# A hybrid attention and FFN block on one core: squares of one x tile divided anew, output projection through scratch tiles, merge gates at a later place

## The chip, the cores and the metric

The kernel runs on 1 core of one Trainium2 chip. The metric is the time of one execution on the device in microseconds (us). Before the change the median of 3 runs is 1706.45 us (1705.3 to 1707.63). One more execution was profiled; the times of single instructions come from it. TensorE is called PE in the profile (PEld is its weight load), VectorE DVE, ScalarE ACT, GpSimd POOL, and SP is the engine whose queue issues most of the DMAs.

## The reference

One layer over 256 latent tokens `x` and 256 context tokens `ctx`, all in float32, with a model width of 2048. Cut to what matters:

```python
hc = modulate(rms_norm(ctx, norm1_g), m_ctx[0], m_ctx[1])          # adaLN of the context tokens
h  = modulate(rms_norm(x, norm1_g), m_lat[0], m_lat[1])            # adaLN of the latent tokens
pc = hc @ w_in[:, :KV_WIDTH];  p = h @ w_in                        # keys, values; queries and gates for x only
oa = gqa(qa, ka_all, va_all);  ob = diff_attn(qb, kb_all, vb_all, ...)
merged = sigmoid(ga) * (oa @ w_br_a) + sigmoid(gb) * (ob @ w_br_b)
x2  = x + m_lat[2] * (merged @ w_out)
h2  = modulate(rms_norm(x2, norm2_g), m_lat[3], m_lat[4])
out = x2 + m_lat[5] * ((silu(h2 @ w_ff_gate) * (h2 @ w_ff_up)) @ w_ff_down)
```

`rms_norm(x)` is `x * rsqrt(mean(x*x) + eps) * g`, and the `m_...` are the six chunks of `silu(c) @ w_ada + b_ada`.

## The kernel before, in words

**Products.** Each weight tile (128x1024 float32, called `wraw`) is split into a high part `whi` (rounded to fp32r by a cast on ScalarE, L227) and a low part `wlo` (the rest, a subtraction on VectorE, L229). Each product is three matmuls (`mm3`, L233 to L235): activation high with weight high, high with low, low with high. There are 7 `wraw` buffers and 3 each of `whi` and `wlo`; a `wraw` buffer comes free when VectorE has made the low part, and SP then issues the next load into it. The instructions of an engine run in the order in which they stand in its queue. The order is decided before the run by a scheduler that works from the program's order and from `issue_after(...)`, which holds an instruction back behind a named one.

**First stage.** Tokens come as four tiles of 128x2048: tile 2 and 3 are x, 0 and 1 are ctx. `row_norm(i)` (L126) sums the squares of a tile: ScalarE squares the middle half (128x1024, L130), VectorE the first and the last quarter (128x512 each, L133); VectorE adds the sums (L136), GpSimd raises them to the power -0.5 (L137), VectorE scales the first 128 columns (L139). TensorE turns these columns (`turn_first`, `xtp`, L351), ScalarE applies scale and shift and so makes the high part of the first activation tile (L364), VectorE the low part (L365, L366), and `kv_first` multiplies it with the first rows of w_in (L374, L375, L377). `hold(cg)` splits the weights for that. `keep_busy(n)` (L345) issues n transposes of the identity whose result nobody reads. Behind the first stage, blocks of the adaLN vectors (`ada`, L290) alternate with matmul groups: an `ada` sum is copied (`asb`, L294), turned (`atp`, L299), and gives scale and shift for the next activation tiles (L331 to L335).

**Merge.** The gates were multiplied out during attention and parked in DRAM (`gate_d`). For each of four column groups `cg`, `load_gated` loads them (`gin`), puts them through a sigmoid on ScalarE (L912) and multiplies (L915), while `project(w_bra, ...)` runs its eight steps of two weight tiles' rows; `take(gates, 1)` moves the generator on by one in each step. In the first column group the end of attention still runs: `o` (L790, copied at L784), and `o_parts(3)`, which makes the last `oT` tiles (L238, L239).

**Output projection.** `out_evac(cg)` takes the two finished token tiles: `y = ps * a2` (L966), `y += xr` (L967), the square sum on ScalarE (L969), and a write of y to DRAM (`x2_d`, L970, GpSimd's queue). y stands in the tile `xn`. `scaled` (L982) then multiplies y by the row `s2`, in place for column groups 0 to 2 and into a scratch tile `z` for group 3; it is called three steps into the next projection. `norm2` applies the row norm to all four quarters (L991), TensorE turns them (`htp`, L996), and the FFN begins. In column group 3 the first six weight tiles of the FFN's gate are loaded and split as well (`first_weights`, into `wbig` tiles or `whi` and `wlo`).

## Time and profile before

| | |
|---|---|
| median of 3 runs | 1706.45 us |
| lowest, highest | 1705.3, 1707.63 us |
| the profiled execution | 1708.76 us |
| its span, first to last instruction | 1707.0 us |
| TensorE busy | 1683.8 us (99%) |
| VectorE, ScalarE, GpSimd busy | 1146.4, 768.8, 201.0 us |
| DMA | 413.15 MB, mean 242 GB/s |
| mean granted TensorE clock | 0.998 |

The profiled execution lies 1.76 us above its span and 2.31 us above the median. In rows of a timeline the first number is the start in us from the span's start, the second the duration; then engine, line, operation, what it writes and reads, how many; in brackets the idle time of the engine before it and who ended that. A row of a table of windows gives the window, its length, the busy time of PE, PEld, DVE, ACT and POOL (with the instruction count), the granted clock, the busy share of the DMA engines, and GB/s.

### The profile page before, as it was taken

The page shows a single profiled execution, that of the slowest core. Times are in us where ns is not written, and L with a number is a line of the kernel's source. Part 1 is how long each engine was busy: PE and PEld are TensorE (multiplying, and loading weights), DVE is VectorE, ACT ScalarE, POOL GpSimd, SP SyncE. Part 2 cuts the span into 40 slices and gives each one's busy share as a digit, 9 for nine tenths or more (in the row PEclk, how much of TensorE's full clock was granted, in tenths as well). Part 3 has the DMA queues.
Part 4 walks back from the last instruction along what each step waited for, and adds up shares of the span by engine and source line. Part 5 has one row for each costly group of instructions (what it writes and reads, how often), then busy time and mean ns, then how long its engine had stood idle before and what let it go on. Part 6 is the DMA issues. An engine that isn't in the chain of part 4 may idle for free.

```text
span 1707.0 us, 21494 instructions
## 1 busy us (share of the span) xinstructions
PE 1683.8 (99%) x7893; PEld 1354.3 (79%) x7893; DVE 1146.4 (67%) x1460; ACT 768.8 (45%) x1037; POOL 201.0 (12%) x295
## 2 busy tenths in 40 slices
PE   7999999999999999999999999999999999999999
PEld 4677778887887778887888788888888888888887
DVE  4764779788788878996666755566666666554554
ACT  4222223246656556577544544444444444433332
POOL 0200002011031110001111101111111111100000
PEclk9999999999999999999999999999999999999999
DMA  8787795678757668676787857788888888765662
GB/s 322 271 294 271 260 338 168 211 260 264 249 177 219 224 225 281 234 246 205 249 270 234 294 173 222 226 268 270 263 268 270 265 273 255 237 221 192 217 209 89
DMA packets 180139, 413.15 MB, mean 242 GB/s; under 512 B 14880, under 2 KB 16112, under 8 KB 179776
## 3 DMA queue, kind: packets, MB, share of 16 engines
q1 hardware_dynamic: 167760, 374.23, 67.0%
q0 software_dynamic: 12272, 37.53, 7.2%
q8 instruction: 62, 1.02, 0.2%
q14 instruction: 45, 0.37, 0.1%
HBM read 395.42 MB, written 16.29 MB: 241 GB/s over the span
## 4 chain that ended last, share of the span: by engine, by line
PE 88%; DVE 5%; DMA 2%; ACT 2%; issue 2%; POOL 0%; SPq 0%; DVEq 0%; ACTq 0%
PE mm L233 27%; PE mm L234 27%; PE mm L235 27%; PE ada L290 2%; DVE wlo L229 1%; DMA wraw<-in_w_in_dram 1%; PE ptp L769 1%; PE o L790 1%; ACT whi L227 1%; PE s L745 1%; ACT p L694 1%; DVE nr L483 0%; DMA wada<-in_ada_t_dram 0%; DMA gate_d<-gate 0%; DVE mx L691 0%
## 5 line engine op out<-in xcount | busy, mean ns | idle before, releaser
L229 DVE TENSOR_TENSOR wlo<-wraw,whi 128x1024 fp32r<-128x1024 f32 x498 | 607.2, 1221 | 420.6 <-ACT whi L227 419.6
L227 ACT CAST whi<-wraw 128x1024 fp32r<-128x1024 f32 x498 | 523.1, 1051 | 730.5 <-PE mm L235 593.1
L234 PE MATMUL mm<-wlo,hT 128*128 128x512 f32 x684 | 266.2, 389 | 0.1
L233 PE MATMUL mm<-whi,hT 128*128 128x512 f32 x684 | 266.1, 389 | 0.0
L235 PE MATMUL mm<-whi,hT 128*128 128x512 f32 x684 | 266.1, 389 | 0.0
L233 PE MATMUL mm<-whi,xT 128*128 128x512 f32 x630 | 251.8, 403 | 1.1 <-DVE vb L418 0.4
L234 PE MATMUL mm<-wlo,xT 128*128 128x512 f32 x630 | 246.9, 392 | 1.0 <-DVE wlo L229 1.0
L235 PE MATMUL mm<-whi,xT 128*128 128x512 f32 x630 | 246.1, 391 | 0.0
L435 DVE SCALAR_TENSOR_TENSOR ada<-wada,vt,ada 128x1024 f32<-128x1024 f32 x120 | 152.1, 1278 | 0.0
L234 PEld LDWEIGHTS mm<-wlo,hT 128*128 128x128 f32 x684 | 128.4, 188 | 27.3 <-DVE wlo L229 0.5
L233 PEld LDWEIGHTS mm<-whi,hT 128*128 128x128 f32 x684 | 128.4, 188 | 26.7
L235 PEld LDWEIGHTS mm<-whi,hT 128*128 128x128 f32 x684 | 128.4, 188 | 26.3
L233 PEld LDWEIGHTS mm<-whi,xT 128*128 128x128 f32 x630 | 117.8, 188 | 38.5 <-issue 10.8
L234 PEld LDWEIGHTS mm<-wlo,xT 128*128 128x128 f32 x630 | 118.5, 188 | 26.0 <-DVE wlo L229 2.9
L235 PEld LDWEIGHTS mm<-whi,xT 128*128 128x128 f32 x630 | 118.3, 188 | 25.2
L233 PE MATMUL mm<-whi,fT 128*128 128x512 f32 x354 | 137.5, 388 | 0.5 <-DVE y L1088 0.5
L235 PE MATMUL mm<-whi,fT 128*128 128x512 f32 x354 | 137.3, 388 | 0.0
L234 PE MATMUL mm<-wlo,fT 128*128 128x512 f32 x354 | 137.3, 388 | 0.0
L233 PEld LDWEIGHTS mm<-whi,fT 128*128 128x128 f32 x354 | 66.4, 188 | 15.0 <-issue 0.8
L235 PEld LDWEIGHTS mm<-whi,fT 128*128 128x128 f32 x354 | 66.4, 188 | 13.8
L234 PEld LDWEIGHTS mm<-wlo,fT 128*128 128x128 f32 x354 | 66.5, 188 | 13.7
L233 PE MATMUL mm<-whi,oT 128*128 128x512 f32 x192 | 75.9, 396 | 0.0
(242 smaller groups left out, 2148.1 us busy)
## 6 DMA issues: line engine op xcount, KB each, us to landing
wraw<-in_w_in_dram SPq DMA_DIRECT2D x159, 512.0 KB, 4.8
wada<-in_w_ada_dram SPq DMA_DIRECT2D x128, 512.0 KB, 4.8
wraw<-in_w_ff_gate_dram SPq DMA_DIRECT2D x88, 512.0 KB, 4.6
wraw<-in_w_ff_up_dram SPq DMA_DIRECT2D x88, 512.0 KB, 5.2
wraw<-in_w_ff_down_dram SPq DMA_DIRECT2D x88, 512.0 KB, 4.7
wada<-in_ada_t_dram SPq DMA_DIRECT2D x64, 512.0 KB, 6.1
wraw<-in_w_br_a_dram SPq DMA_DIRECT2D x32, 512.0 KB, 5.2
wraw<-in_w_out_dram SPq DMA_DIRECT2D x32, 512.0 KB, 5.2
```

The lines of the kernel that those rows point to most:

```text
L227: last_hi.append(nc.scalar.copy(out=hi[:, 0:nk], in_=raw[:, 0:nk]))
L229: last_lo.append(nc.vector.tensor_tensor(out=lo[:, 0:nk], in0=raw[:, 0:nk], in1=hi[:, 0:nk].bitcast(F32), op=ALU.subtract))
L233: nc.tensor.matmul(ps, lhsT=ah, rhs=wh, start=first, stop=False, skip_group_check=skip)
L234: nc.tensor.matmul(ps, lhsT=ah, rhs=wl, start=False, stop=False, skip_group_check=skip)
L235: return nc.tensor.matmul(ps, lhsT=al, rhs=wh, start=False, stop=last, skip_group_check=skip)
L290: last_pe[0] = nc.tensor.matmul(aps[32 * g:32 * g + 32, 0:ncol], lhsT=cst[:, k, :], rhs=rhs, start=(k < 4), stop=(k >= NKT - 4))
L435: nc.vector.scalar_tensor_tensor(out=dst, in0=wt, scalar=sc[:, 0, kt:kt + 1], in1=dst, op0=ALU.mult, op1=ALU.add)
L694: nc.scalar.activation(out=p, in_=sp, func=AF.Exp, bias=mx, accum_out=rs)
L745: nc.tensor.matmul(sps[i], lhsT=qT[rows, x, hh, tk * P:(tk + 1) * P], rhs=kT["b", grp][y][rows, hh, :], start=(n == 0), stop=(n == 2))
L769: nc.tensor.transpose(out=tp[:, kt * P:(kt + 1) * P], in_=p[:, kt * P:(kt + 1) * P], identity=ident)
L790: nc.tensor.matmul(op[:, 0:BV], lhsT=pT[:, kt, :], rhs=vb[:, kt, hh * BV:(hh + 1) * BV], start=(kt == 0), stop=(kt == 3))
```

## The change

1. **First stage.** `row_norm` is divided into `squares_act`, `squares_dve` and the rest. For tiles 2, 0 and 1 the same pieces are squared by the same engines as before. For tile 3 (the second x tile) ScalarE squares the last three quarters (128x1536) and VectorE only the first (128x512); this one is held behind the low part of `hold(2)`, and the low part of `hold(4)` behind it. The second `keep_busy(6)` after the first products becomes `keep_busy(4)`.
2. **Merge.** In column group 0 the sigmoids are held behind the last copy of `o` (a new list `last_o`) and not behind the last high part, and the generator of the gates is moved on by 0, 0, 0, 0, 2, 2, 3, 0 in the eight steps of the projection. The other column groups are as before.
3. **Output projection.** y stands in a scratch tile (tag `nr`, 2 buffers) and not in `xn`; `scaled` reads it and writes `xn`, in all four column groups, 4 ticks after the evacuation for groups 0 to 2 and at once for group 3. `z` goes; `norm2` reads and writes `xn` alone. The square's unused output takes a buffer of tag `sq`.

The change moves instructions at three places that the prediction speaks of. The rows are those of an engine's queue, in order; the numbers in the names tell tiles apart.

The first place is the first stage. On VectorE, `wlo_210` belongs to `hold(2)`, `wlo_214` (now `wlo_216`) to `hold(4)`, `tok3` is the second x tile, `junk` takes the squares that nobody reads, `sums` holds the sums of squares, and `vb0` takes the product of column group 4 for the first x tile. Before:

```order
L229 TENSOR_TENSOR wlo_210<-wraw_181,whi_209 128x1024
L229 TENSOR_TENSOR wlo_214<-wraw_183,whi_213 128x1024
L133 SCALAR_TENSOR_TENSOR junk_245,sums_90<-tok3_185 128x512
L133 SCALAR_TENSOR_TENSOR tok3_185,sums_90<-tok3_185 128x512
L136 TENSOR_REDUCE sums_90<-sums_90 128x1
L382 COPY vb0_105<-mm_227 128x512
L139 TENSOR_SCALAR tok3_185<-tok3_185,sums_90 128x128
```

and after:

```order
L235 TENSOR_TENSOR wlo_210<-wraw_181,whi_209 128x1024
L136 SCALAR_TENSOR_TENSOR junk_213,sums_90<-tok3_185 128x512
L235 TENSOR_TENSOR wlo_216<-wraw_183,whi_215 128x1024
L142 TENSOR_REDUCE sums_90<-sums_90 128x1
L145 TENSOR_SCALAR tok3_185<-tok3_185,sums_90 128x128
L388 COPY vb0_105<-mm_230 128x512
```

One square of `tok3` is gone from VectorE, the other stands ahead of the second low part, and the scaling of `tok3` stands ahead of the copy into `vb0`. On ScalarE, further on in the same stage, `asb_534` (now `asb_531`) is the 256 columns wide `ada` sum of the block after next, and `xT0` and `cT` are the high parts that the next matmul group multiplies. Before:

```order
L227 CAST whi_562<-wraw_560 128x512
L294 COPY asb_450<-ada_429 128x128
L334 ACTIVATE xT0_205<-hx_459,mod0_426 128x256
L334 ACTIVATE cT_458<-hx_463,mod0_426 128x256
L294 COPY asb_534<-ada_509 128x256
```

and after:

```order
L233 CAST whi_559<-wraw_557 128x512
L300 COPY asb_447<-ada_426 128x128
L300 COPY asb_531<-ada_506 128x256
L340 ACTIVATE xT0_205<-hx_456,mod0_423 128x256
L340 ACTIVATE cT_455<-hx_460,mod0_423 128x256
```

The copy of this sum has moved ahead of the two high parts. Its two transposes `atp` have moved likewise on TensorE, from behind the 60 matmuls that follow to a place ahead of them.

The second place is the merge, on ScalarE, in column group 0. `gin` are the gates under the sigmoid, `pT` the turned attention weights, `o1` the last attention output, `oT3` its high part, and the three `whi` are those of steps 3 to 5 of the projection (counted from 0). Before:

```order
L912 ACT_TABLE_LOAD
L912 ACTIVATE gin_7261<-gin_7261 128x512
L238 CAST pT_7177<-ptp_7213 128x4x128
L238 CAST pT_7177<-ptp_7220 128x4x128
L912 ACTIVATE gin_7283<-gin_7283 128x512
L227 CAST whi_7311<-wraw_7309 128x1024
L784 COPY o1_6782<-o_7247 128x512
L227 CAST whi_7331<-wraw_7329 128x1024
L238 CAST oT3_7303<-o1_6782 128x1024
L912 ACTIVATE gin_7327<-gin_7327 128x512
L227 CAST whi_7353<-wraw_7351 128x1024
L912 ACTIVATE gin_7349<-gin_7349 128x512
```

and after:

```order
L233 CAST whi_7297<-wraw_7295 128x1024
L244 CAST pT_7174<-ptp_7210 128x4x128
L244 CAST pT_7174<-ptp_7217 128x4x128
L233 CAST whi_7319<-wraw_7317 128x1024
L796 COPY o1_6779<-o_7242 128x512
L924 ACT_TABLE_LOAD
L924 ACTIVATE gin_7315<-gin_7315 128x512
L244 CAST oT3_7292<-o1_6779 128x1024
L924 ACTIVATE gin_7337<-gin_7337 128x512
L233 CAST whi_7344<-wraw_7342 128x1024
L924 ACTIVATE gin_7360<-gin_7360 128x512
L924 ACTIVATE gin_7364<-gin_7364 128x512
```

Two high parts of weights have moved ahead of the table load and the first two sigmoids; the table load and a sigmoid now stand between the copy of `o1` and `oT3`, and the other two sigmoids behind the high part of step 5.

The third place is the output projection, on VectorE, where column group 2 is evacuated and group 3 runs. `wbig` are the weight tiles that are split into large tiles, the last three of them weights of the FFN. Before:

```order
L229 TENSOR_TENSOR wlo_8502<-wraw_8499,whi_8501 128x1024
L229 TENSOR_TENSOR wbig_8557<-wraw_8555,wbig_8557 128x1024
L229 TENSOR_TENSOR wlo_8522<-wraw_8519,whi_8521 128x1024
L982 TENSOR_TENSOR xn0_7943<-xn0_7943,s2_8293 128x512
L982 TENSOR_TENSOR xn1_7944<-xn1_7944,s2_8293 128x512
L229 TENSOR_TENSOR wlo_8534<-wraw_8531,whi_8533 128x1024
L229 TENSOR_TENSOR wbig_8568<-wraw_8566,wbig_8568 128x1024
L229 TENSOR_TENSOR wlo_8546<-wraw_8543,whi_8545 128x1024
L229 TENSOR_TENSOR wbig_8588<-wraw_8586,wbig_8588 128x1024
L229 TENSOR_TENSOR wbig_8593<-wraw_8591,wbig_8593 128x1024
L229 TENSOR_TENSOR wbig_8598<-wraw_8596,wbig_8598 128x1024
L966 TENSOR_TENSOR xn0_7943<-mm_8461,a2_8457 128x512
```

and after:

```order
L235 TENSOR_TENSOR wlo_8505<-wraw_8502,whi_8504 128x1024
L983 TENSOR_TENSOR xn0_7940<-y2_8446,s2_8294 128x512
L983 TENSOR_TENSOR xn1_7941<-y2_8454,s2_8294 128x512
L235 TENSOR_TENSOR wlo_8525<-wraw_8522,whi_8524 128x1024
L235 TENSOR_TENSOR wbig_8560<-wraw_8558,wbig_8560 128x1024
L235 TENSOR_TENSOR wlo_8537<-wraw_8534,whi_8536 128x1024
L235 TENSOR_TENSOR wbig_8571<-wraw_8569,wbig_8571 128x1024
L235 TENSOR_TENSOR wlo_8549<-wraw_8546,whi_8548 128x1024
L235 TENSOR_TENSOR wbig_8591<-wraw_8589,wbig_8591 128x1024
L235 TENSOR_TENSOR wbig_8596<-wraw_8594,wbig_8596 128x1024
L235 TENSOR_TENSOR wbig_8601<-wraw_8599,wbig_8601 128x1024
L976 TENSOR_TENSOR y2_8582<-mm_8464,a2_8460 128x512
```

The two multiplications by `s2` (into `xn0`, `xn1`) have moved up by two rows of weights, and read `y2`.

The diff:

```diff
         last_pow.append(nc.gpsimd.tensor_tensor(out=r, in0=r, in1=neghalf[:, 0:n], op=ALU.pow))
         return r
-    def row_norm(i, late=None):
-        xt = tok_in[i]
-        mid, end = xt[:, CG:3 * CG], xt[:, 3 * CG:]
-        with tc.issue_after(late[0].ins) if late else nullcontext():
+    def squares_act(i, c0=CG, c1=3 * CG, late=None):
+        mid = tok_in[i][:, c0:c1]
+        with tc.issue_after(late.ins) if late else nullcontext():
             nc.scalar.activation(out=mid, in_=mid, func=AF.Square, scale=D ** -0.5, accum_out=ssq[:, i, 0:1])
-        with tc.issue_after(late[1].ins) if late else nullcontext():
-            for n, (src, dst) in enumerate(((xt[:, 0:CG], scratch("junk", tag="p", bufs=4)), (end, end))):
-                nc.vector.scalar_tensor_tensor(out=dst, in0=src, scalar=1.0 / D, in1=src, op0=ALU.mult, op1=ALU.mult,
-                                               accum_out=ssq[:, i, 1 + n:2 + n])
+
+    def squares_dve(i, parts=(0, 3), late=None):
+        with tc.issue_after(late.ins) if late else nullcontext():
+            for n, q in enumerate(parts):
+                src = tok_in[i][:, q * CG:(q + 1) * CG]
+                dst = src if q else scratch("junk", tag="p", bufs=4)
+                held = nc.vector.scalar_tensor_tensor(out=dst, in0=src, scalar=1.0 / D, in1=src, op0=ALU.mult, op1=ALU.mult,
+                                                      accum_out=ssq[:, i, 1 + n:2 + n])
+        return held
+
+    def row_norm(i):
         r = r_tok[:, i:i + 1]
         nc.vector.tensor_reduce(out=r, in_=ssq[:, i, :], axis=AX.X, op=ALU.add)
         last_pow.append(nc.gpsimd.tensor_tensor(out=r, in0=r, in1=neghalf[:, 0:1], op=ALU.pow))
-        xt = xt[:, 0:P]
+        xt = tok_in[i][:, 0:P]
         nc.vector.tensor_scalar(out=xt, in0=xt, scalar1=r, scalar2=None, op0=ALU.mult)
     r_of = []
...
     BATCH = ((), (1, 4), (0, 1, 2, 3), (0, 1, 2, 3), (0, 1, 2, 3), ())
     steps = STEPS
+    squares_act(2)
+    squares_dve(2)
     row_norm(2)
     turn_first(2)
     keep_busy(6)
...
     keep_busy(6)
     mod_first(2)
     hold(2, (last_asb[-1], last_first[-1]))
-    hold(4, (first_hi[-1], last_first[-1]))
+    hold(4, (first_hi[-1], squares_dve(3, (0,), last_lo[-1])))
+    squares_act(3, CG, 4 * CG, last_hi[-1])
     kv_first(2, (2, 3))
     kv_first(2, (4, 5))
-    keep_busy(6)
+    keep_busy(4)
     for tok, todo in ((3, ((2, (0,)), (3, (2, 3)), (3, (4, 5)), (3, (0,)))),
                       (0, ((0, (2, 3)), (0, (4, 5)), (0, (0,)))), (1, ((1, (2, 3)), (1, (4, 5)), (1, (0,))))):
-        row_norm(tok, (last_hi[-1], last_lo[-1]))
+        if tok < 2:
+            squares_act(tok, late=last_hi[-1])
+            squares_dve(tok, late=last_lo[-1])
+        row_norm(tok)
         with tc.issue_after(last_pe[0].ins):
             turn_first(tok)
         mod_first(tok)
...
         nc.vector.scalar_tensor_tensor(out=p0, in0=p0, scalar=r0, in1=p1, op0=ALU.mult, op1=ALU.add)
         return [p0]
-    pair = []
+    pair, last_o = [], []
     def back(br, u, pr):
...
             for kt in range(4):
                 vh, vl = [v[:, kt, grp * AD:(grp + 1) * AD] for v in v_a]
                 mm3(op, vh, vl, pT[0][:, kt, :], pT[1][:, kt, :], kt == 0, kt == 3)
-            nc.scalar.copy(out=o_raw(grp * 4 + hh - 1, 2), in_=op)
+            last_o.append(nc.scalar.copy(out=o_raw(grp * 4 + hh - 1, 2), in_=op))
             return
         vb = acc["vb"][grp].rearrange("p (t c) -> p t c", c=CG)
         tk = u % 2
...
                     g = scratch("gin", tag="p", bufs=4)
                     nc.gpsimd.dma_start(out=g, in_=gate_d[w, tk, :, cg * CG:(cg + 1) * CG])
                     yield None
-                    with tc.issue_after(last_hi[-1].ins):
+                    with tc.issue_after((last_hi if cg else last_o)[-1].ins):
                         nc.scalar.activation(out=g, in_=g, func=AF.Sigmoid)
                     if w == 1:
                         with tc.issue_after(last_lo[-1].ins):
...
                 if k == 3:
                     assert not work
                     o_parts(3)
-            take(gates, 1)
+            take(gates, 1 if cg else (0, 0, 0, 0, 2, 2, 3, 0)[k])
     drain(later)
     b_all = ada_everywhere("b_all", 2)
...
         nc.gpsimd.dma_start(out=r, in_=row_d[i, cg:cg + 1, :].partition_broadcast(P).rearrange("p l d -> p (l d)"))
         return r
-    s_of = {}
-
     def out_evac(cg):
         a2 = row_piece("a2", 0, cg)
-        s_of[cg] = row_piece("s2", 1, cg)
+        s2 = row_piece("s2", 1, cg)
         def f(tk, ps):
             xr = scratch("xr", tag="p", bufs=4)
             nc.gpsimd.dma_start(out=xr, in_=t["x"][0, tk * P:(tk + 1) * P, cg * CG:(cg + 1) * CG])
-            y = xn[tk][:, cg * CG:(cg + 1) * CG]
+            y = scratch("y2", tag="nr", bufs=2)
             nc.vector.tensor_tensor(out=y, in0=ps, in1=a2, op=ALU.mult)
             nc.vector.tensor_tensor(out=y, in0=y, in1=xr, op=ALU.add)
-            junk = scratch("junk_x")
+            junk = scratch("junk_x", tag="sq", bufs=2)
             nc.scalar.activation(out=junk, in_=y, func=AF.Square, accum_out=ssx[tk][:, cg:cg + 1])
             nc.gpsimd.dma_start(out=x2_d[tk, :, cg * CG:(cg + 1) * CG], in_=y)
-            if cg == 3:
-                scaled(tk, 3)
+
+            def scaled():
+                nc.vector.tensor_tensor(out=xn[tk][:, cg * CG:(cg + 1) * CG], in0=y, in1=s2, op=ALU.mult)
+
+            if cg < 3:
+                after(4, scaled)
+            else:
+                scaled()
         return f
     hT = Parts("hT", NKT)
-    rows, last_norm = {}, []
-
-    def scaled(tk, q):
-
-        y = xn[tk][:, q * CG:(q + 1) * CG]
-        rows[tk, q] = scratch("z") if q == 3 else y
-        nc.vector.tensor_tensor(out=rows[tk, q], in0=y, in1=s_of[q], op=ALU.mult)
+    last_norm = []
     def norm2(tk):
...
         nc.vector.tensor_reduce(out=ss, in_=ssx[tk], axis=AX.X, op=ALU.add)
         r = rstd_of(ss, 1, D, "rstd2")
         for q in range(4):
-            h = rows[tk, q]
+            h = xn[tk][:, q * CG:(q + 1) * CG]
             nc.vector.scalar_tensor_tensor(out=h, in0=h, scalar=r, in1=b_all[:, q * CG:(q + 1) * CG], op0=ALU.mult, op1=ALU.add)
         yield None
         for q in range(4):
             tp = tp_ps("htp") if q % 2 == 0 else s_ps("htp")
             for j in range(4):
-                nc.tensor.transpose(out=tp[:, j * P:(j + 1) * P], in_=rows[tk, q][:, j * P:(j + 1) * P], identity=ident)
+                nc.tensor.transpose(out=tp[:, j * P:(j + 1) * P], in_=xn[tk][:, q * CG + j * P:q * CG + (j + 1) * P], identity=ident)
             hi, lo = hT.four(q, tk * P, P)
             last_norm.append(split(hi, lo, tp.rearrange("p (h q) -> p h q", h=4)))
             yield None
...
             take(norm2_of[1], 2)
     for cg in range(4):
-        gen = project(w_out, mT, NKT, cg * CG, out_evac(cg), **(dict(tail=TURN2, hook=tail_hook, in_big=(6, 7)) if cg == 3 else {}))
-        take(gen, 3)
-        if cg:
-            for tk in range(2):
-                scaled(tk, cg - 1)
-        drain(gen)
+        drain(project(w_out, mT, NKT, cg * CG, out_evac(cg), **(dict(tail=TURN2, hook=tail_hook, in_big=(6, 7)) if cg == 3 else {})))
     NFT = DFF // P
```

## The prediction

> **What bounds the kernel now.** The first line of the profile's page, busy time by engine, says that little is left:
>
> ```profile
> PE 1683.8 (99%) x7893; PEld 1354.3 (79%) x7893; DVE 1146.4 (67%) x1460; ACT 768.8 (45%) x1037; POOL 201.0 (12%) x295
> ```
>
> TensorE is busy for 1683.8 of 1707.0 us. A change that leaves the matmuls alone can win only its 23.2 us of idle time, and time in which its clock is low. So I read the windows around TensorE's waits at the places of the change. Columns: window, length, busy time of PE, PEld, DVE, ACT, POOL, granted clock, DMA share, GB/s.
>
> ```profile
> 20.38:23.84 3.46, 1.60 (x11) 1.04 (x9) 2.34 (x9) 1.72 (x5) 0.55 (x1) 1.00 1.06 410
> 48.29:48.58 0.29, 0.00 (x1) 0.01 (x1) 0.11 (x2) 0.29 (x2) 0.00 (x0) 1.00 1.28 325
> 62.82:63.13 0.31, 0.31 (x3) 0.14 (x1) 0.31 (x2) 0.00 (x0) 0.00 (x0) 1.00 0.18 53
> 802.58:803.47 0.89, 0.00 (x2) 0.03 (x1) 0.89 (x3) 0.89 (x3) 0.46 (x1) 1.00 0.79 276
> 964.40:968.00 3.60, 2.21 (x9) 1.21 (x8) 3.60 (x4) 1.62 (x2) 0.55 (x1) 1.00 1.01 358
> ```
>
> TensorE idles 1.86 us in the first stage, 0.89 in the merge and 1.39 in the output projection. The second and third rows belong to a side effect, below. The last reading is the granted clock, in windows of the first stage:
>
> ```profile
> 14.87:18.28 3.41, 2.21 (x16) 1.40 (x11) 1.78 (x6) 3.03 (x5) 0.00 (x0) 1.00 1.01 398
> ...
> 21.69:25.10 3.41, 1.59 (x6) 1.17 (x7) 2.39 (x6) 2.28 (x5) 0.39 (x1) 1.00 1.04 399
> 25.10:28.51 3.41, 3.41 (x9) 2.65 (x8) 2.14 (x8) 1.85 (x4) 0.55 (x1) 0.50 1.02 410
> ```
>
> From 25.10 to 28.51 us the clock is 0.50 while TensorE has work throughout: 3.41 us at half speed lose 1.70. In the stretch of equal length ahead of it TensorE was busy for 1.59 us (47%); a stretch with 2.21 (65%) did not lower the clock. The waits there are thus paid twice. [...]
>
> **The change part by part.**
>
> *First stage, VectorE.* Its rows around the second x tile (`tok`), then TensorE's and ScalarE's:
>
> ```profile
> 17.61 2.35 DVE L229 TENSOR_TENSOR wlo<-wraw,whi 128x1024 fp32r<-128x1024 f32 x2
> 19.88 0.69 DVE L133 SCALAR_TENSOR_TENSOR junk<-tok 128x512 f32<-128x512 f32 x1
> ...
> 21.29 0.16 DVE L136 TENSOR_REDUCE sums<-sums 128x1 f32<-128x4 f32 x1
> 21.36 0.68 DVE L382 COPY vb<-mm 128x512 f32<-128x512 f32 x1
> 22.11 0.29 DVE L139 TENSOR_SCALAR tok<-tok,sums 128x128 f32<-128x128 f32 x1
> ```
>
> ```profile
> 20.37 0.62 PE L377 MATMUL mm<-wlo,xT 128*128 128x512 f32 x2
> 20.83 0.81 PE L345 MATMUL idle<-ident 128*128 128x128 f32 x6
> 22.46 0.33 PE L351 MATMUL xtp<-ident,tok 128*128 128x128 f32 x1 [0.81 <-DVE tok L139]
> 23.84 0.50 PE L374 MATMUL mm<-whi,xT 128*128 128x512 f32 x1 [1.05 <-ACT whi L227]
> ```
>
> ```profile
> 17.75 1.06 ACT L130 ACTIVATE tok<-tok 128x1024 f32<-128x1024 f32 x1
> 18.72 0.19 ACT L130 ACTIVATION_READ_ACCUMULATOR tok<-tok 128x1 f32 x1
> 19.42 1.07 ACT L384 COPY kb<-mm 128x512 f32<-128x512 f32 x2 [0.52 <-PE mm L377]
> ```
>
> Of two squares VectorE keeps one. It lies between the low parts, so the second low part ends 0.69 later, at 20.65 and not 19.96, and the sum can start there and not at 21.29: 0.64 earlier. Scaling and `xtp` follow as before (0.82 and 0.35 behind), so `xtp` starts at 21.82 and everything that follows it, up to L374 now at 23.84, is 0.64 earlier. TensorE must be free by then: its two L377 wait for the second low part until 20.7 (0.33 late), and four idle transposes take 0.59 instead of 0.81, so they end at 21.75. The copy into `vb`, now behind the scaling, waits for nothing new and ends before VectorE's next step, which waits for ScalarE anyway. On ScalarE 1.5 times 1024 columns cost at most 1.59 instead of 1.06; the 0.53 lie in the 0.52 us for which it waits ahead of the copies at 19.42, so I cost them at nothing (0.1 if that wait were gone). Together **-0.64**, between -0.3 (if the late L377 weighed in full) and -0.8.
>
> *First stage, clock.* The 1.86 us of waits shrink to 0.33 for the low part, some 0.07 ahead of `xtp`, and the unchanged 1.05: 1.45. The worst 3.41 us stretch then has 1.96 of work, 57%, between the 47% that lowered the clock and the 65% that did not. I take it that the clock stays up, being the nearer bound: **-1.70** in an execution like the profiled one; the other end is 0.
>
> *First stage, a side effect.* The copy of the 256 columns wide sum now stands ahead of two high parts on ScalarE.
>
> ```profile
> 48.02 0.51 ACT L334 ACTIVATE xT<-hx,mod 128x256 fp32r<-128x256 f32 x1 [1.74 <-DVE hx L331]
> 48.43 0.49 ACT L334 ACTIVATE cT<-hx,mod 128x256 fp32r<-128x256 f32 x1
> 48.83 0.35 ACT L294 COPY asb<-ada 128x256 f32<-128x256 f32 x1
> ```
>
> It waits for TensorE's sums, which end at 48.29 (start of the idle window above). Then the copy runs, and the high part `xT` starts at about 48.6, not 48.02. The matmuls behind it, and VectorE's low parts, which now also have the reduction of the transposes ahead of them, start some 0.59 later. The two transposes fit into that wait, so their 0.31 us at 62.82 are saved: net **+0.28**, between 0 and +0.6.
>
> *Merge.* ScalarE's rows, and one of TensorE:
>
> ```profile
> 798.85 1.28 ACT L912 ACT_TABLE_LOAD   x1
> 801.36 0.63 ACT L912 ACTIVATE gin<-gin 128x512 f32<-128x512 f32 x1 [1.23 <-DMA gin<-gate_d]
> ...
> 806.97 0.59 ACT L784 COPY o<-o 128x512 f32<-128x512 f32 x1 [2.55 <-PE o L235]
> 807.45 1.05 ACT L227 CAST whi<-wraw 128x1024 fp32r<-128x1024 f32 x1
> 808.40 1.05 ACT L238 CAST oT<-o 128x1024 fp32r<-128x1024 f32 x1
> 809.35 0.64 ACT L912 ACTIVATE gin<-gin 128x512 f32<-128x512 f32 x1
> ```
>
> ```profile
> 812.66 0.39 PE L234 MATMUL mm<-wlo,oT 128*128 128x512 f32 x1
> ```
>
> Before, the table load and the wait for the gate's transfer hold ScalarE, and behind them `pT`, for which TensorE waits 0.89. This wait goes. What is late next? The table load now stands behind the copy of `o`, which TensorE releases at about 806.3 (0.89 earlier than so far, but 0.23 later since its last matmul now follows one more of the projection's; two L377 take 0.62, one L234 0.39). Then come the copy 0.48, table load 1.28, sigmoid 0.6, `oT` 0.95, sigmoid 0.6, the high part of step 5 1.05 and its low part on VectorE 1.2, which ends at about 812.5. TensorE wants this low part in L234, at 812.66 so far and at 811.77 with the gain: it waits 0.73. Net **-0.16**, between 0 and -0.89. The first gate's transfer has landed by 801.36, long before its sigmoid at 808.1. Its buffer comes free 6.7 us later than before, and so the next column group's first gate is loaded later on GpSimd's queue; it is used a column group later.
>
> *Output projection.*
>
> ```profile
> PE mm L234 <- DVE wlo L229: 1.4, 2, 0.8
> ```
>
> ```profile
> DVE xn L982 <- DMA x_d<-xn: 4.7, 3, 2.6
> ```
>
> TensorE waits 1.4 us for low parts, which wait on VectorE behind `scaled`, which may not overwrite y before its write to DRAM has landed. With y in a scratch tile the multiplications wait only for `s2`, loaded a column group ahead; the next column group's evacuation, which takes the same two scratch tiles, waits for the write, but comes a whole column group after it. The 1.39 goes. Next come the FFN's weights and the last evacuation:
>
> ```profile
> 967.22 1.05 ACT L227 CAST wbig<-wraw 128x1024 fp32r<-128x1024 f32 x1 [1.98 <-DMA wraw<-in_w_ff_gate_dram]
> 968.50 1.05 ACT L227 CAST wbig<-wraw 128x1024 fp32r<-128x1024 f32 x1 [0.23 <-DMA wraw<-in_w_ff_gate_dram]
> 972.07 0.69 DVE L966 TENSOR_TENSOR xn<-mm,a 128x512 f32<-128x512 f32 x1 [0.88 <-PE mm L235]
> ```
>
> VectorE must finish the tile cast at 968.50 (until 969.55, low part until 970.75) before the evacuation, which TensorE would allow at 972.07 - 1.39 = 970.68. So 0.07 is given back: **-1.3**. SP issues this tile's load one low part later than before, about 1.2 us, but it lands 1.28 behind its predecessor while the DMA engines are full (share 1.01), so it follows in their queue. If it did come 1.2 us later, nearly all would be lost: bounds 0 and -1.39.
>
> *Sum* against the profiled execution: -0.64 - 1.70 + 0.28 - 0.16 - 1.3 = -3.52, 1708.76 to 1705.24. That execution is 2.31 above the median. It had the low window; the runs, 2.33 apart, look like a mixture of executions with it and without (1.70 apart). Without it the sum is -1.82. For the median run I take half of 1.70: -2.67, 1706.45 to **1703.8**.
>
> **The rivals.**
>
> 1. *The clock gives nothing.* If the windows of the clock run freely, two executions of one program can differ in whether both waits fall into one window, and the median run before had none low. Then 1706.45 - 1.82 = 1704.6. For it: 1705.3 among the runs. [...] Chance 0.18.
> 2. *All of it.* The median run had the low window, and the table load costs nothing because step 5's low part comes in time: -3.52 - 0.73, 1702.2. Against it: 0.73 us of shortage. Chance 0.17.
> 3. *The output projection gives its gain back*, the third FFN tile landing later with its issue: -2.67 + 1.3, 1705.1. Chance 0.11.
> 4. *Slower.* With four idle transposes instead of six, and TensorE's new wait of 0.33, stretches at 57% lower the clock even where before nothing fell, and a second low window follows because half-speed work starves the next products: 1706.45 - 1.82 + 2 x 1.70 = 1708.0. It decides if the threshold lies above 57%; the 65% row leaves room for that, but the low window at 25.10 was followed by full speed. Chance 0.04.
>
> **How the numbers follow.** My forecast, 1703.8, has 0.50. A measurement of this kernel can tell about 0.2%, 3.4 us, from no change; that limit is 1703.04. The forecast's own bounds (the side effect 0 to +0.6, the merge 0 to -0.89, the clock's half up or down) reach across it in a fifth of its cases: 0.10, and with rival 2, 0.27 for faster. Slower by 0.2% would need four low windows: 0.03. The rest, 0.70, is within. The range takes in rivals 1 to 3 with some of their spread: 1702.0 to 1705.8.
>
> **What would show it.** In the new profile: the reduction of the second x tile's sums about 0.6 us earlier, and clock 1.00 from 15 to 32 us; ScalarE's 256 columns wide `asb` ahead of `xT`, and TensorE idle for 0.9 us ahead of the matmuls that follow; no wait for `pT` in the merge, but one for the low part of step 5, near 0.7 us; no wait of `scaled` for `x_d`, and no idle TensorE between the last evacuation's projection and `htp`. I am wrong if a low clock remains in the first stage, if the merge's wait does not return, or if TensorE waits ahead of `htp`.

## The result, and the profile after

The changed kernel takes 1703.57 us (median of 16 runs, 1702.09 to 1706.29), the kernel before, run beside it, 1706.96 (16 runs, 1704.09 to 1709.17): a ratio of 0.9982, with a 95% interval from 0.9975 to 0.999. The forecast was 1703.8, within 1702.0 to 1705.8. The profiled execution takes 1705.82, with a span of 1704.0; it is the third longest of the 16. One run of a kernel below (`both_fills`) took 2357.05 us at a granted clock of 0.672 and is left out of its median and ratio. The page of the profiled execution begins:

```profile
PE 1682.3 (99%) x7891; PEld 1353.4 (79%) x7891; DVE 1145.6 (67%) x1458; ACT 768.0 (45%) x1037; POOL 201.0 (12%) x295
```

The span is 3.0 us shorter (1707.0 before). To see where, I took the starts of the same matmuls in both traces. In the table a minus means that the changed kernel is ahead:

| place in the profile before, us | 16.97 | 31.54 | 64.02 | 611.89 | 640.13 | 794.91 | 829.91 | 955.11 | 1000.03 | end |
|---|---|---|---|---|---|---|---|---|---|---|
| lead of the changed kernel, us | -1.16 | -2.10 | -1.95 | -1.56 | +0.16 | 0.00 | -1.03 | -1.03 | -2.64 | -2.94 |

The first stage's lead is all gone before the merge. So the agreement of the medians needs a closer look, stage by stage.

*First stage.* VectorE in the changed kernel, then TensorE (L380 there is L374 before):

```profile
17.58 0.69 DVE L136 SCALAR_TENSOR_TENSOR junk<-tok 128x512 f32<-128x512 f32 x1
...
18.19 1.22 DVE L235 TENSOR_TENSOR wlo<-wraw,whi 128x1024 fp32r<-128x1024 f32 x1
19.52 0.16 DVE L142 TENSOR_REDUCE sums<-sums 128x1 f32<-128x4 f32 x1
```

```profile
20.68 0.33 PE L357 MATMUL xtp<-ident,tok 128*128 128x128 f32 x1
22.07 0.50 PE L380 MATMUL mm<-whi,xT 128*128 128x512 f32 x1 [1.05 <-ACT whi L233]
...
27.25 0.41 PE L296 MATMUL ada<-wada,cst 128*32 128x128 f32 x2 [0.77 <-DMA wada<-in_ada_t_dram]
```

The first product stands at 15.81 us (16.97 before), and L380 at 22.07 (L374 at 23.84): 6.26 behind it, not 6.87. That is 0.61 earlier, for a forecast of 0.64. But at 27.25 a wait of 0.77 stands that the profile before did not have: TensorE waits for the transfer of the next weights of the conditioning (`wada`). The clock stays up; two stretches of 3.41 us follow, laid out in whole steps from 619.25, where the granted clock of this execution falls (the length of a step is measured in the last section). Such a stretch is called a window of the clock below:

```profile
15.09:18.50 3.41, 2.24 (x7) 1.34 (x8) 2.83 (x7) 2.13 (x4) 0.00 (x0) 1.00 1.02 392
18.50:21.92 3.42, 2.40 (x11) 1.23 (x9) 2.33 (x5) 3.30 (x8) 0.56 (x1) 1.00 1.02 417
```

*The copy of `asb`.* ScalarE and TensorE:

```profile
46.31 0.37 ACT L300 COPY asb<-ada 128x256 f32<-128x256 f32 x1 [2.13 <-PE ada L296]
46.58 0.51 ACT L340 ACTIVATE xT<-hx,mod 128x256 fp32r<-128x256 f32 x1
```

```profile
44.70 1.50 PE L296 MATMUL ada<-wada,cst 128*32 128x256 f32 x22
46.73 0.44 PE L305 MATMUL atp<-ident,asb 128*128 128x128 f32 x2 [0.54 <-ACT asb L300]
47.14 0.50 PE L239 MATMUL mm<-whi,xT 128*128 128x512 f32 x1
```

The sums end at 46.20 (44.70 + 1.50) and L239 starts 0.94 behind them (0.29 before), as the prediction has it.

*A low clock where the change has nothing.* Two of the clock's windows around 619 us, then TensorE there:

```profile
615.84:619.25 3.41, 1.20 (x8) 0.79 (x8) 2.95 (x6) 0.41 (x1) 1.53 (x1) 1.00 0.79 241
619.25:622.66 3.41, 3.41 (x11) 2.83 (x12) 3.41 (x6) 2.85 (x7) 0.00 (x0) 0.50 0.97 354
```

```profile
616.36 0.60 PE L781 MATMUL ptp<-ident,p 128*128 128x128 f32 x4
619.17 1.08 PE L781 MATMUL ptp<-ident,p 128*128 128x128 f32 x4 [2.21 <-DVE on L807]
```

This wait for VectorE is in the profile before too (1.90 us at 618.5). There it lay across two windows (615.61 to 619.02 with 2.91 us of work, 619.02 to 622.43 with 2.01, granted clock 1.00 in both and behind them); here it fell into one, which had 35% of work, and 3.41 us at a granted clock of 0.50 followed. The stretch from 611.89 to 640.13 took 29.96 instead of 28.25, and the first stage's lead was lost here.

*Merge.* ScalarE, VectorE, TensorE of the changed kernel:

```profile
806.16 0.59 ACT L796 COPY o<-o 128x512 f32<-128x512 f32 x1 [1.46 <-PE o L241]
806.76 1.28 ACT L924 ACT_TABLE_LOAD   x1
...
810.07 1.03 ACT L233 CAST whi<-wraw 128x1024 fp32r<-128x1024 f32 x1
```

```profile
811.13 1.23 DVE L235 TENSOR_TENSOR wlo<-wraw,whi 128x1024 fp32r<-128x1024 f32 x1 [0.24 <-ACT whi L233]
```

```profile
811.40 0.39 PE L239 MATMUL mm<-whi,oT 128*128 128x512 f32 x1
811.63 0.39 PE L240 MATMUL mm<-wlo,oT 128*128 128x512 f32 x1
```

The low part ends at 812.36, near the 812.5 forecast. But the matmul at 811.63, the one that stood at 812.66 before, does not wait for it: it runs while this low part is still being made, so it reads the one ahead of it. The wait of 0.73 does not come.

*Output projection.* The two waits for low parts are gone. The third FFN tile (ScalarE), VectorE behind it, and `htp`:

```profile
967.42 1.05 ACT L233 CAST wbig<-wraw 128x1024 fp32r<-128x1024 f32 x1 [0.76 <-DMA wraw<-in_w_ff_gate_dram]
```

```profile
968.51 1.23 DVE L235 TENSOR_TENSOR wbig<-wraw,wbig 128x1024 fp32r<-128x1024 f32 x1 [0.59 <-ACT wbig L233]
969.65 0.68 DVE L976 TENSOR_TENSOR y<-mm,a 128x512 f32<-128x512 f32 x1
```

```profile
974.77 1.23 PE L1006 MATMUL htp<-ident,xn 128*128 128x128 f32 x8 [0.22 <-DVE xn L1001]
```

The evacuation starts straight behind this low part, and TensorE waits 0.22 ahead of `htp`.

### The profile page after: what moved, and what is told of

It reads as the page before. It is cut to its first block, busy times and chain, and to the rows that moved or that the text cites. A ratio compares the mean times of both kernels' runs of the same rounds, so it can differ in the third digit from the quotient of the medians.

```text
span 1704.0 us, 21492 instructions
## 1 busy us (share of the span) xinstructions
PE 1682.3 (99%) x7891; PEld 1353.4 (79%) x7891; DVE 1145.6 (67%) x1458; ACT 768.0 (45%) x1037; POOL 201.0 (12%) x295
## 4 chain that ended last, share of the span: by engine, by line
PE 91%; DVE 4%; DMA 3%; issue 1%; ACT 1%; POOL 0%; SPq 0%; DVEq 0%; ACTq 0%; POOLq 0%
PE mm L239 28%; PE mm L240 27%; PE mm L241 27%; PE ada L296 2%; PE ptp L781 1%; DVE wlo L235 1%; DMA tok<-in_x_dram 1%; PE o L802 1%; DMA wraw<-in_w_in_dram 1%; PE s L757 1%; DMA wada<-in_ada_t_dram 1%; ACT whi L233 0%; DMA wraw<-in_w_ff_gate_dram 0%; PE o L239 0%; PE s L239 0%
## 5 line engine op out<-in xcount | busy, mean ns | idle before, releaser
L239 PE MATMUL mm<-whi,hT 128*128 128x512 f32 x684 | 266.1, 389 | 0.0
L239 PE MATMUL mm<-whi,xT 128*128 128x512 f32 x630 | 252.4, 404 | 1.0 <-DVE vb L424 1.0
L239 PEld LDWEIGHTS mm<-whi,hT 128*128 128x128 f32 x684 | 128.4, 188 | 26.7
L239 PEld LDWEIGHTS mm<-whi,xT 128*128 128x128 f32 x630 | 118.2, 189 | 38.1 <-issue 13.4
L239 PE MATMUL mm<-whi,fT 128*128 128x512 f32 x354 | 137.5, 388 | 0.5 <-DVE y L1093 0.5
L239 PEld LDWEIGHTS mm<-whi,fT 128*128 128x128 f32 x354 | 66.5, 188 | 15.3 <-issue 0.8
L239 PE MATMUL mm<-whi,oT 128*128 128x512 f32 x192 | 75.9, 396 | 0.0
```

What stands on the lines that cost most here:

```text
L239: nc.tensor.matmul(ps, lhsT=ah, rhs=wh, start=first, stop=False, skip_group_check=skip)
```

## The experiments

Every kernel gives a trace of its own, and the three stages do not touch one another. So I read each trace for all of them, between the same matmuls, beside the ratio of the times. Intervals are 95%; beside each set of experiments the kernel before ran again (33, 23, 21 and 15 runs).

**The kernel before once more, and each part alone.** `before_again` is the kernel before without an edit.

> The kernel before, once more, for its clock. The prediction took half of 1.70 us, that is, the low clock between 25 and 28.5 us in about half of the executions: then this profile shows it or not, and the runs fall into two groups 1.7 us apart, those with a granted clock of 0.998 above those with 0.999 or 1.000. Theory now: the low window comes in any execution wherever a wait of 1.5 us or more falls whole into one of the clock's 3.41 us stretches (25 us in the profile before, 619 us in the profile after); then the times of the runs spread over 4 us without two groups, and the ratio is 1.000.

Measured: 1706.25 us (11 runs), ratio 0.9994 (0.9985 to 1.0003). Its runs spread over 3.1 us (1704.45 to 1707.59) without two groups. Its span is 1703.8 where the first profile had 1707.0, with the same code. Its window around 21 us, then the two of `only_merge`, whose first stage is also the old one:

```profile
19.25:22.66 3.41, 1.87 (x11) 1.23 (x9) 2.33 (x8) 1.68 (x4) 0.55 (x1) 1.00 1.02 413
```

```profile
20.44:23.85 3.41, 1.57 (x10) 1.04 (x9) 2.29 (x8) 2.20 (x4) 0.55 (x1) 1.00 1.04 404
23.85:27.26 3.41, 3.41 (x10) 2.67 (x9) 2.77 (x9) 2.10 (x6) 0.00 (x0) 0.50 1.03 410
```

With the same waits a window holds 55% of work in one execution (1.87 us) and 46% in another (1.57), and only the latter is followed by a low clock, of 0.50. Four traces have the unedited old first stage (`before`, `before_again`, `only_merge`, `only_out`): two have the low window (the one at half clock), two have not.

`only_first` has the first stage's lines alone:

```
-    hold(4, (first_hi[-1], last_first[-1]))
+    hold(4, (first_hi[-1], squares_dve(3, (0,), last_lo[-1])))
+    squares_act(3, CG, 4 * CG, last_hi[-1])
...
-    keep_busy(6)
+    keep_busy(4)
```

> The kernel before with the first stage's part alone (squares and four idle transposes). Prediction: -0.64 +0.28 in every execution and -1.70 in half of them, -1.2 us, ratio 0.9993, and -2.1 where the kernel before had the low window. Theory now: the stage itself ends 0.6 to 2 us earlier, but the lead is given back to waits for transfers and at the wait of 2 us near 617 us, so that the end comes 0 to 0.6 earlier: ratio 0.9996 to 1.0000.

Measured: 1706.1 us, ratio 0.9993 (0.9984 to 1.0002), too wide to tell the two theories apart. The trace tells more, in the table below, and so do the granted clocks: none of its 11 runs reports 0.998 or less, where 4 of 11 of `only_merge`, 3 of 11 of `only_out` and 14 of the 33 of the kernel before beside them do.

`only_merge` (it fills `last_o` too):

```
-                    with tc.issue_after(last_hi[-1].ins):
+                    with tc.issue_after((last_hi if cg else last_o)[-1].ins):
...
-            take(gates, 1)
+            take(gates, 1 if cg else (0, 0, 0, 0, 2, 2, 3, 0)[k])
```

> The kernel before with the merge's part alone (the first column group's gates later). Prediction: -0.16 us, ratio 0.9999, with a new wait of 0.73 us for the low part of step 5 near 812 us. Theory now: the low part is used a step later than the prediction read, so the wait does not come and the whole wait goes: -0.9 to -1.1, ratio 0.9994.

Measured: 1705.08 us, ratio 0.9994 (0.9984 to 1.0004); from 796 to 830 us its trace has no wait of TensorE.

`only_out`:

```
-            y = xn[tk][:, cg * CG:(cg + 1) * CG]
+            y = scratch("y2", tag="nr", bufs=2)
...
-                scaled(tk, 3)
+            if cg < 3:
+                after(4, scaled)
+            else:
+                scaled()
```

> The kernel before with the output projection's part alone (y in a scratch tile). Prediction: -1.3 us, ratio 0.9992. Rival of the prediction: nothing, the third FFN tile landing later. Theory now: each of the two waits costs its idle time and another 0.26 us in which the matmuls start up again (starts 1.16 and 0.33 apart instead of 0.23 and 0.23), so -1.9, less 0.2 given back behind them: -1.7, ratio 0.9990.

Measured: 1705.62 us, ratio 0.9991 (0.9982 to 1.0). Its waits for low parts are gone, but a new one is there. VectorE, and TensorE:

```profile
966.21 1.23 DVE L229 TENSOR_TENSOR wbig<-wraw,wbig 128x1024 fp32r<-128x1024 f32 x1 [0.81 <-ACT wbig L227]
967.35 0.68 DVE L964 TENSOR_TENSOR y<-mm,a 128x512 f32<-128x512 f32 x1
```

```profile
972.47 1.23 PE L994 MATMUL htp<-ident,xn 128*128 128x128 f32 x8 [1.24 <-DVE xn L989]
```

The third tile came later than in the changed kernel's trace (14.31 us behind the matmul at 955.11, there 13.34), and the evacuation with it: what the prediction's third rival said.

**The changed kernel once more, with filler, and with a load less.** `after_again` is the changed kernel without an edit.

> The changed kernel once more, for its stages. Theory: no low clock in the first stage; the matmuls that the profile before has at 31.5 us come at 29.4 to 29.7, as in executions of the kernel before without the low window (29.4 and 29.7 in two), since the wait for the next weights of the conditioning (0.3 to 1.0 us) takes the 0.6 us that the squares gave; stage from 795 to 830 us 34.0 instead of 35.0 to 35.4. From 955 to 980 us between 23.2 and 24.2, with a wait of 0 to 1.2 ahead of htp. Ratio to the kernel before 0.998. Rival: the 0.6 us stay, and 31.5 is reached at 28.8 to 29.1.

Measured: 1704.5 us, ratio 0.9985 (0.9976 to 0.9994); 31.54 reached at 29.53.

`both_fills`:

```
-    keep_busy(4)
+    keep_busy(10)
...
-            for kt in range(4):
+            for kt in list(range(4)) * (4 if (br, u, i) == ("a", 0, 0) else 1):
```

> The changed kernel with ten idle transposes instead of four behind the early products, and the first four transposes of p of the first a unit done four times over (12 more) in the wait near 617 us. Theory of the covered lead: the six transposes (0.66 us) lie in the 0.5 to 0.8 us for which TensorE waits for the conditioning's weights, so 31.5 is reached at 29.4 to 29.7 as without them; the copy asb falls back behind the high parts, so 31.5 to 64 takes 32.4 and not 32.7; the 12 transposes lie in a wait of 1.3 to 2.2 us, and the share of work there rises from 35 to 66% to over 70%, so that no low window comes before the end. Median 0.3 to 0.6 below the changed kernel's, ratio to the kernel before 0.9977, and the slowest run 1705 or less. Rival: six transposes cost 0.66, ratio 0.9984 or more.

Measured: 1703.91 us (11 runs), ratio 0.9984 (0.9976 to 0.9993), nothing that differs from `after_again`. The first half holds: 31.54 is reached at 29.38 although six more transposes are there, `asb` falls back behind the high parts, and 31.54 to 64.02 takes 32.30. The window of the wait near 617 us, and the wait:

```profile
613.63:617.04 3.41, 2.37 (x20) 2.00 (x19) 2.95 (x6) 0.20 (x1) 1.53 (x1) 1.00 0.86 285
```

```profile
613.95 1.91 PE L781 MATMUL ptp<-ident,p 128*128 128x128 f32 x16
616.89 0.66 PE L781 MATMUL ptp<-ident,p 128*128 128x128 f32 x4 [1.04 <-DVE on L807]
```

It holds 69% of work, just short of the 70% expected, and no low clock follows. Some 2 of its 2.37 us of work are transposes; without them it would hold under 0.5 us, and behind 1.20 us the clock of the profile after fell, so in this trace transposes counted as work for the clock. One of its runs took 1707.3, so the slowest run did not come down to 1705 as expected.

`third_tile`:

```
         for x in xs:
-            raw = wp.tile(...)
-            nc.sync.dma_start(out=raw, ...)
+            if x != 2:
+                raw = wp.tile(...)
+                nc.sync.dma_start(out=raw, ...)
```

> The changed kernel with the FFN's third weight tile made from the second one's raw weights: one load less, so the FFN's products of that tile are of the wrong weights, with the same instructions otherwise. Theory: the wait ahead of htp (0.2, 0.8 and 1.2 us where the waits of the output projection were short) comes from the third tile's landing, behind which VectorE's low part and the last evacuation stand; without the load 955 to 980 us takes 22.8 to 23.0 instead of 23.3 to 24.2, and htp waits for nothing. Rival: the chain from the last evacuation to htp is too long by itself; then htp still waits 0.2 to 1.2.

Measured in one execution: 1703.79 us. No wait of TensorE stands between 960 and 990 us, but 955.11 to 980 takes 23.27, not 22.8 to 23.0. VectorE:

```profile
964.96 2.36 DVE L235 TENSOR_TENSOR wbig<-wraw,wbig 128x1024 fp32r<-128x1024 f32 x2 [0.85 <-ACT wbig L233]
967.24 0.68 DVE L976 TENSOR_TENSOR y<-mm,a 128x512 f32<-128x512 f32 x1
```

Two low parts now run back to back, and the evacuation still comes straight behind them. So VectorE's queue is the floor under this stretch. That the tile's landing sets the wait at `htp`, one execution without the load does not show, as `after_again` with it has next to none either (0.12 us); for that stand the five traces at the end, in which the wait grows with the landing.

`before_fill`:

```
             hold(0, (first_hi[-1], last_first[-1]))
+            keep_busy(8)
```

> The kernel before with eight more idle transposes behind the second tile's, in the wait of 1.05 us for the high part. Theory: the stretch that had 46% of work in two of three executions has 65% or more, no low clock comes in the first stage, and 31.5 us is reached at 29.4 to 29.9, as by the changed kernel: the clock is all that the first stage's part is worth. Rival: the squares' 0.64 count as well, and 31.5 is reached 0.6 later than by the changed kernel, at 30.1 or later.

Measured in one execution: 1709.23 us, with 71% of work in the window from 21.62, no low clock in the whole program, and 31.54 reached at 29.92. That is at the edge between the two theories. It started late, with the first product at 16.96; of six traces with the changed first stage the one that started as late (17.03, `third_tile`) got there at 29.38. So 0.5 of the squares' 0.64 may count where the start is late, by one trace of each. A time of 1709.23 with the clock up shows that the low windows are not all of the spread: the wait near 617 us lasted 3.15 us in it, 1.33 to 2.46 in the other traces without filler there.

**The third tile's place, and the clock without idle transposes.** `evac_first` (`last_xn` collects the norm's multiplications, which make `xn`):

```
-                first_weights(range(3), True, (last_hi[-3], last_lo[-3]))
+                first_weights(range(2), True, (last_hi[-3], last_lo[-3]))
             take(norm2_of[tk], 1)
             if tk == 0:
+                first_weights((2,), True, (last_hi[-1], last_xn[-1]))
```

> The changed kernel with the FFN's third weight tile emitted behind the normalised rows: on VectorE its low part now follows the last evacuation and the four multiplications of the norm. Theory: the low part of this tile, late by its transfer, is what keeps the last evacuation and so htp back; then no execution waits for htp, 955 to 980 us takes 22.9 to 23.3 instead of 23.3 to 24.5, the FFN does not wait for the tile (980 to 1300 us 319.7, as before), and the ratio to the kernel before is 0.9981 (0.3 us below the changed kernel). Rival: the FFN's first steps then wait for the low part, and what 955 to 980 gains comes back behind it.

Measured: 1704.41 us, ratio 0.9987 (0.9978 to 0.9996). `htp` waits for nothing, and the time up to 980 falls to 22.63. The rival holds all the same. VectorE, and the FFN's third matmul:

```profile
975.11 1.22 DVE L235 TENSOR_TENSOR wlo<-wraw,whi 128x1024 fp32r<-128x1024 f32 x1
976.25 1.28 DVE L245 TENSOR_TENSOR hT<-htp,hT 128x512 fp32r<-128x512 f32 x2
```

```profile
976.99 0.50 PE L241 MATMUL mm<-wbig,hT 128*128 128x512 f32 x1 [0.76 <-DVE hT L245]
```

The low parts that were moved now stand ahead of `hT`'s, and 955.11 to 1000.03 takes 43.89.

`ten_evac` is the same with `keep_busy(10)` for `keep_busy(4)`.

> The same with ten idle transposes instead of four in the first stage. Theory: as both_fills showed, the six more lie in the wait for the conditioning's weights, and the copy asb falls back behind the high parts, so 31.5 us is reached at 29.4 to 29.7 and 31.5 to 64 takes 32.3 instead of 32.7; with the output projection's 0.3 to 0.5 that is 0.7 below the changed kernel, ratio to the kernel before 0.9978. Rival: nothing that can be measured, 0.9985.

Measured: 1705.51 us, ratio 0.9996 (0.9987 to 1.0005), an interval that holds neither the theory's 0.9978 nor the rival's 0.9985. The copy `asb` is behind again, 31.54 is reached at 29.73, and 31.54 to 64.02 takes 32.55, so the stages are much as expected; why the time is 1.1 us above `evac_first`'s is left open.

`no_idle`:

```
-    keep_busy(6)
     mod_first(2)
...
-    keep_busy(4)
```

> The changed kernel without the idle transposes ahead of the second and of the third x tile (six and four). Theory: the clock falls to half behind any stretch of 3.41 us with less than half of its time in work (46, 46, 35 and 49% did it, 50, 50 and 55% did not); without the transposes (0.8 and 0.6 us of work) the stretches of 65 to 70% between 15 and 22 us fall to 42 to 50%, and a low window comes between 18 and 26 us; 28.5 us is then reached 1.6 later than the start alone would have it. Rival: only an idle stretch lowers the clock, and nothing falls here, as TensorE never rests for a whole stretch.

Measured in one execution: 1705.18 us. Windows:

```profile
14.40:17.81 3.41, 1.62 (x18) 0.79 (x11) 1.61 (x6) 2.85 (x5) 0.00 (x0) 1.00 1.02 378
17.81:21.22 3.41, 3.41 (x9) 2.43 (x8) 2.74 (x6) 2.30 (x4) 0.55 (x1) 0.50 1.03 418
```

The low window comes where it was expected, behind 47% of work. The cost is not 1.6: the way from the first product to 28.51 took 9.85 instead of the 9.15 to 9.38 of the traces with four transposes there, and 31.54 was reached at 29.55 as without it. Most of the half-speed work filled time in which TensorE would have waited.

`tile_late`:

```
-            first_w[x] = split_w(raw, WK, in_big, behind)
+            raws2[x] = raw
+            if x != 2:
+                first_w[x] = split_w(raw, WK, in_big, behind)
...
             if i == last - 1:
+                first_w[2] = split_w(raws2[2], WK, True, (last_hi[-1], last_norm[-1]))
```

> The changed kernel with the third FFN tile loaded where it was, but cast and subtracted behind the first two high and low parts of hT. Theory: the last evacuation no longer stands behind this tile's low part, and hT's low part not either (for which the matmuls waited 0.76 us in evac_first), so no wait stands at htp or in the FFN's first steps, and 955 to 1000 us takes 42.7 to 43.0, where the changed kernel took 43.3 to 44.5 and evac_first 43.9; 0.5 to 1 us below the changed kernel, ratio to the kernel before 0.998. Rival: the FFN now waits for the third tile itself, and 955 to 1000 stays at 43.3 or more.

Measured: 1703.73 us, ratio 0.9985 (0.9976 to 0.9994); 955.11 to 1000.03 takes 43.63. `htp` still waits 0.2, since the fourth tile's low part (1.23 us at 970.84) now stands between the evacuation and the norm. The FFN does not wait for the third tile, and still nothing is won; what else holds this stretch at 43.6 is left open. No version that I tried beats the changed kernel.

**All traces together**, between the same matmuls (places of the profile before):

| | with the old code | with the new code |
|---|---|---|
| 31.54 reached at, no low window | 29.42, 29.71 | 29.65, 29.44, 29.53, 29.38, 29.13, 29.40 |
| the same, with the low window | 31.54, 30.95 | none |
| 31.54 to 64.02 (`asb` behind, ahead) | 32.48, 32.27, 32.71, 32.17, 32.44 | 32.72, 32.63, 32.85, 32.63, 32.75, 33.00 |
| 794.91 to 829.91 | 35.00, 35.42, 35.07, 35.07, 35.41 | 33.97 to 34.04 in nine traces |
| 955.11 to 1000.03 | 44.92, 43.78, 44.70, 44.83, 44.08 | 44.27, 43.31, 43.40, 44.51, 43.46 |

(In the first three rows kernels with another number of idle transposes are left out, but for `before_fill`, the last of the old in row three; in the last row those that move the third tile or leave out its load. What counts as old or new code is the stage's own.)

And the runs, by the granted clock that each reports (0.001 of it is 1.7 us, half of one window of 3.41 us). Of the kernel before there are 102, its own and `before_again`'s, one with a clock of 0.948 left out; of the changed kernel 27:

| granted clock | kernel before: runs, median us | changed kernel: runs, median us |
|---|---|---|
| 0.997 and 0.998 | 36, 1708.0 | 1, 1706.1 |
| 0.999 | 46, 1706.2 | 13, 1704.5 |
| 1.000 | 20, 1704.7 | 13, 1703.5 |

The mean clock rises from 0.9988 to 0.9994, which is 1.1 us of 1704. Over all kernels, 43 of 124 runs with the old first stage report 0.998 or less, and 8 of 82 with the new one. Seven of these 8 are among the 22 runs of `evac_first` and `ten_evac`, whose traces show no low window before the program's last; where the clock fell in those runs is not known.

## Why the prediction was right, and where it was not

The time was right, in part by luck: of its five terms two were right in size, one was offset by another stretch, and two were mis-sized in opposite directions, and what they were off by cancels. Two of the three signs by which I said that I would be wrong came: the merge's wait did not return, and TensorE waits ahead of `htp`.

*First stage, VectorE (-0.64).* The step itself was right: 0.61. The mistake lies in what stands behind it, which the prediction did not look at: the lead runs into the next weights of the conditioning (a wait of 0.77 us in the trace after, 0.4, 0.5 and 1.0 in three others, none in `third_tile` and `evac_first`). Without a low window 31.54 is reached at 29.57 on average with the old code (two traces, 0.3 apart) and at 29.42 with the new (six, 0.5 apart): **-0.15**, too little to tell from nothing.

*Clock (-1.70, halved to -0.85 for the median).* Right, and for the reason given: of four traces of the old first stage two have the low window, of six traces of the new one none. It does not hang on where the windows fall: the worst stretch of 3.41 us between 14 and 30 us, wherever it begins, has 45 to 46% of work in the four traces of the old stage and 60 or 61% in the six of the new one (57% was forecast). The runs' clocks give **-1.1** for the whole program, an upper bound, as a low window in which TensorE would have waited costs less than its 1.7 us (0.5 to 0.7 in `no_idle`). The two shares taken, 47% where the clock fell and 65% where it stayed up, are closer together in the traces (below). The prediction missed that the same can happen at another wait: the profiled execution lost 1.7 us at 617, on a wait that the change does not touch (none of the other 13 traces has a low window there). Rival 1, by which the clock gives nothing, falls, but its condition, windows that lie elsewhere in another execution, is what makes the halving right. The low windows begin at 25.10 (before), 23.85 (`only_merge`), 17.81 (`no_idle`) and 619.25 us (after), that is 1.21, 3.37, 0.74 and 1.44 us past a whole number of steps of 3.4133 from the span's start: no two of these four executions have their windows at the same place.

*Side effect (+0.28).* Right: 32.76 instead of 32.41 from 31.54 to 64.02, **+0.35**. It hangs on the number of idle transposes: with ten of them the scheduler puts `asb` behind again, and 32.30 and 32.55 were measured.

*Merge (-0.16).* Mis-sized: 33.99 instead of 35.19, **-1.2**. The step that failed is "TensorE wants this low part in L234, at 812.66". I had paired the low part ending at 812.63 with the matmul that started 0.03 later. In the trace after that matmul runs ahead of this low part's end; it wants the part a step (12 matmuls, 2.7 us) later. I said that I would be wrong if the wait did not return, and it did not. Also too small was the wait's price, as in the next point.

*Output projection (-1.3).* Mis-sized the other way: 43.79 instead of 44.46, **-0.7**. Two errors lie in it. This wait costs more than its idle time. TensorE in the profile before:

```profile
964.18 0.39 PE L235 MATMUL mm<-whi,mT 128*128 128x512 f32 x1
964.41 0.39 PE L233 MATMUL mm<-whi,mT 128*128 128x512 f32 x1
965.57 0.50 PE L234 MATMUL mm<-wlo,mT 128*128 128x512 f32 x1 [0.77 <-DVE wlo L229]
965.90 0.40 PE L235 MATMUL mm<-whi,mT 128*128 128x512 f32 x1
```

Matmuls in a row start 0.23 apart here (964.18 to 964.41); these start 1.16 and 0.33 apart, so that the wait of 0.77 costs 1.04. That alone would have made the term larger. But "it follows in their queue" was right on the order and wrong on the time: the third tile's cast starts 12.87 to 14.56 us behind the place of 955.11 in five executions of the new code (12.87, 13.34, 13.52, 14.31, 14.56, in the order `after_again`, after, `no_idle`, `only_out`, `both_fills`), and the wait at `htp` grows with it: 0.12, 0.22, 0.52, 1.24, 1.56. So rival 3, at 0.11, came in two of the five, and in part in a third. That the tile lands later because its load is issued later is not shown: in five traces of the old code its cast starts 12.90 to 14.29 behind the same matmul, and in the one at 14.29 (`only_first`) `htp` waits 0.75 too. The landing moves from one execution to the next, and the old code's waits for low parts lie ahead of it.

*The sum.* -0.15 - 1.1 + 0.35 - 1.2 - 0.7 = -2.8; all runs together have medians of 1706.6 (119) and 1703.8 (27), -2.8. The forecast's -2.67 was right because the merge was worth 1.0 and the clock 0.25 more, and the first stage and the output projection together 1.1 less, than it said. That these errors cancel is luck. In the profiled pair the sum came about in yet another way: 1.16 of the lead at 16.97 is only how that execution started (the first product stands between 15.78 and 17.03 in all traces, with either code), and the low clock at 617 took it back.

## What to carry to other kernels

When a wait goes, follow the freed engine to its next transfer: a lead that ends at a landing is no lead, and one that moves an engine closer to a late tile brings a new wait. Pair an operand with its reader by what the code needs, not by the nearest start in the trace. This kernel, 99% busy, differs by 6 us between its own executions (1704.03 to 1710.51 us before the change); read a change of 3 from several traces, stage by stage, and from one pair of profiles not at all.

## What the runs showed of the hardware

The traces before and after hold four records of the granted clock each (1.00, 0.50, 1.00, 0.50). Their starts lie 10.240, 3.413 and 1675.944 us apart in the one before, 607.572, 3.413 and 1082.025 in the one after: 3, 1 and 491, and 178, 1 and 317 steps of 3.4133 us (10.240 / 3). These steps are the windows of this document. The first records start at 14.85 and 11.68 us; ahead of them the clock is not recorded.

The clock fell to 0.50 behind windows with 1.20 (after), 1.57 (`only_merge`), 1.59 (before), 1.62 (`no_idle`) and 1.69 us of work (busy time of the profile, in which the ends of matmuls are modelled), the last in the profile before at its end, where TensorE had no work left to slow down:

```profile
1701.04:1704.45 3.41, 1.69 (x13) 1.28 (x11) 1.70 (x4) 0.00 (x0) 0.00 (x0) 1.00 0.21 74
1704.45:1706.98 2.53, 0.00 (x0) 0.00 (x0) 0.00 (x0) 0.00 (x0) 0.00 (x0) 0.50 0.16 55
```

It stayed at 1.00 behind 1.87 (`before_again`), 1.76 (`tile_late`) and, in `only_first`, behind 1.70:

```profile
614.53:617.94 3.41, 1.70 (x11) 1.21 (x9) 2.95 (x6) 0.97 (x1) 1.53 (x1) 1.00 0.84 256
617.94:621.36 3.42, 3.42 (x17) 2.90 (x18) 3.42 (x6) 2.80 (x6) 0.00 (x0) 1.00 0.97 336
```

With the old first stage 31.54 was reached at 30.95 and 31.54 where the clock fell, at 29.42 and 29.71 where it did not: 1.2 to 2.1 us apart, of which half of the 3.41 us can be the clock's. In `no_idle` the way to 28.51 took 0.5 to 0.7 longer, and at 31.54 nothing of it was left (29.55). Two waits of TensorE in the profile before cost some 0.25 us beyond the idle time that the profile gives them: 0.27 in the rows of 964.18 to 965.90, 0.24 at the merge's wait (starts of 802.19, 803.47 and 803.77 around an idle time of 0.89).
